# A decoder trunk's layer norms: last column block of the second rows in two banks, first scaling in halves, constant products taken out

## The chip, the cores and the metric

The kernel runs on one core of one Trainium2 chip. The metric is the device time of one execution in microseconds. An execution that the hardware profiler recorded gives the rows that are quoted below. Engines are called as the profile calls them: PE multiplies matrices, DVE and ACT work elementwise on 128 partitions, POOL does small things here, SP issues the transfers. PE writes into PSUM, which is used here as eight banks of 512 float32 columns.

## The reference

One sequence of 256 rows by 2048 columns goes through two layers. Each layer has a token mixer (forgetting attention in layer 0, sliding-window attention in layer 1) and a gated convolutional feed-forward part with 5632 inner columns. Around every one of these four parts stands the same frame:

```python
for i in range(DEPTH):                       # 2 layers
    mod = c_act @ ada_w[i] + ada_b[i]
    sh1, sc1, g1, sh2, sc2, g2 = jnp.split(mod[:, None, :], 6, axis=-1)
    h = x * (1.0 + sc1) + sh1
    y = fox_attention(h, ...) if i % 2 == 0 else swa_attention(h, ...)
    x = layer_norm(DEEPNORM_ALPHA * x + (1.0 + g1) * y, ln_mix_g[i], ln_mix_b[i])
    h = x * (1.0 + sc2) + sh2
    y = conv_ffn(h, ...)                     # h @ w_up, causal conv, silu(g) * val, @ w_down
    x = layer_norm(DEEPNORM_ALPHA * x + (1.0 + g2) * y, ln_ffn_g[i], ln_ffn_b[i])
```

The layer norm takes mean and variance over the 2048 columns of a row, so nothing of the next part can start before the last column of the last product of the part before it is known. The change concerns these four places.

## The kernel before

The 256 rows lie as two row tiles of 128 (t = 0 and 1; "the second rows" are t = 1) in a tile `x`. Weights come from memory in pieces of 256 rows by 512 columns, sixteen or more for one column block of a product. ACT casts each piece to a rounded part `wh` (L265), DVE forms the remainder `wl` (L276); `h` and `l` of a piece stand in one of four buffers. Every product is done three times, high by high, high by low and low by high, so the input of a product also comes as two tiles: `hH` (high, by ACT) and `hL` (low, by DVE; the profile names it `hH` as well).

There are two kinds of products. In `x_mm` the rows of the sequence are the stationary operand and 512 weight columns stream; its result is `xs`, one bank for each row tile. In `w_mm` the weights are stationary and 256 sequence rows stream; its result is `ws`. Input columns go by groups k of 128, sixteen in all; a weight piece covers two of them. The last column block of a part that ends in a layer norm uses `x_mm_end`: it finishes the products of the first rows and keeps those of the second rows back for the last two or four pieces, so that the evacuation of t = 0 runs beside the products of t = 1.

`residual` evacuates a column block: gate times product (L625), added to `x` (L627), and bn_stats (L632). After the last block follow bn_aggr (L635), the addition of epsilon (L637) and the power -1/2 on POOL (L638), which gives `rs`. A product of mean and `rs` for t = 0 (L631, on DVE) is the bias for ACT.

`between` stands at three of the four norms, here called seams: after the mixer of layer 0 (about 471 us), after its feed-forward part (about 1215 us) and after the mixer of layer 1 (about 1477 us). The fourth norm ends the kernel: there `residual` is followed by two operations with the norm's weights (L1173, L1174) and the output's transfers. A seam issues, in this order: a few products of constants whose result nobody reads (`spin(o, 3)`), the scaling of the first 512 columns, d = 0, of both rows (`normalise`: t = 0 on ACT, L648, t = 1 on DVE, L650), transposes of columns k = 0 to 3 (`mod_turn`, L489), `mod_pair` for them (high part straight from the bank on ACT, L499; the same affine on DVE, L500; the difference as low part, L501), and `spin(o, 2)`. The other columns come as `feeds`: after each weight piece one more pair of k goes through transposes and `mod_pair` (ACT L503, DVE L504, then the split into high and low at L84 and L85), and at k = 4, 8 and 12 the scaling of the next 512 columns goes ahead. In the forms of the first two feeds the word is `fast`.

Each engine works through its own queue in the order in which it was written by a scheduler. The scheduler may move an instruction ahead or behind others by its estimate of times, except where `pin` keeps it in the order of the program. So the text of the program doesn't tell the order of a queue; the rows of the queues do.

Of the kernel before, what the change touches and what calls it, by code (L numbers as in the profile page):

```python
# [41 lines left out]
def hybrid_trunk(ctx: ExitStack, tc: tile.TileContext, a: dict, out: bass.AP):  # L42
# [22 lines left out]
    def bank(name="sm"):  # L65
        return psp.tile([P, 512], F32, tag="ps", name=name)
# [1 line left out]
    def w_banks():  # L68
        return [bank("ws").rearrange("p (a s) -> p a s", a=2) for _ in range(2)]

    def x_banks():
        return [bank("xs") for _ in range(NT)]

    def mm(o, lhsT, rhs, start=False, stop=False, **kw):
        return nc.tensor.matmul(o, lhsT, rhs, start=start, stop=stop, **kw)  # L75

    def pin(ins, on=True):

        if on:
            tc.keep_in_program_order(ins)  # L80
# [214 lines left out]
    def x_mm_end(ps, stat, nk, n):  # L295

        kept = []

        def use(kc, h, l):
            end = kc >= nk - 2 * n  # L300
            x_mm(ps, kc, h, l, stat, nk - 1, ts=(0,) if end else range(NT))
            if end:
                kept.append((kc, h, l))
            if kc + 2 >= nk:
                for e in kept:
                    x_mm(ps, *e, stat, nk - 1, ts=(1,))

        return use

# [9 lines left out]

    def x_stationary(wsrc, col, k0, nk, stat, end=0):  # L320

        ps = x_banks()
# [148 lines left out]


    hpad = cst.tile([P, 2 * KC * S + 64], F32R, name="hH")
    hH = hL = None

    def place(o):
# [13 lines left out]
            os.append(o)  # L490
        return os

    def mod_pair(G, B, k, ps, fast=False, keep=False):
        tmp = ttile()
        if fast:
            for j in range(2):
                o = tmp[:, j * S:(j + 1) * S]
                g, b = G[:, k + j:k + j + 1], B[:, k + j:k + j + 1]
                pin(nc.scalar.activation(hH[:, k + j, :], ps[j], AF.Identity, bias=b, scale=g), keep)  # L499
                nc.vector.tensor_scalar(o, ps[j], g, b, op0=ALU.mult, op1=ALU.add)  # L500
                nc.vector.tensor_tensor(hL[:, k + j, :], o, f32(hH[:, k + j, :]), op=ALU.subtract)  # L501
            return
        pin(nc.scalar.activation(tmp[:, :S], ps[0], AF.Identity, bias=B[:, k:k + 1], scale=G[:, k:k + 1]), keep)  # L503
        nc.vector.tensor_scalar(tmp[:, S:], ps[1], G[:, k + 1:k + 2], B[:, k + 1:k + 2],  # L504
                                op0=ALU.mult, op1=ALU.add)
        split(hH[:, k:k + 2, :], hL[:, k:k + 2, :], tmp.rearrange("p (j s) -> p j s", j=2))
# [4 lines left out]
    def spin(o, n):  # L511

        for _ in range(n):
            pin(mm(o[:, :3 * P], ident, mask.rearrange("p a b -> p (a b)"), start=True, stop=True))

    def modulate(G, B, norm, o=None):

        def feed(k):
            if k % 4 == 0:
                norm(k // 4)  # L520
            mod_pair(G, B, k, mod_turn(k, 2), k < 4)

        feeds.extend([lambda k=k: feed(k) for k in range(0, KC, 2)])
        for _ in range(2):
            feeds.pop(0)()
        spin(o, 2)

    def opening(plan, proj, prep):

# [83 lines left out]
                prep()  # L613


    stats = cst.tile([P, NT, D // 512, nc.vector.BN_STATS_DIM], F32, name="stats")
    mhalf = cst.tile([P, 1], F32, name="mhalf")
    nc.gpsimd.memset(mhalf, -0.5)

# [2 lines left out]
    def residual(ps, d, gate, last):  # L622
        for t in range(NT):
            tmp = ttile()
            nc.vector.tensor_tensor(tmp, ps[t], gate[:, d * 512:(d + 1) * 512], op=ALU.mult)  # L625
            xs = x[:, t, d * 512:(d + 1) * 512]
            nc.vector.tensor_tensor(xs, xs, tmp, op=ALU.add)  # L627
            if last:
                if t == 1 and d == D // 512 - 1:
                    mu, rs, nm = moments[0]  # L630
                    pin(nc.vector.scalar_tensor_tensor(nm, mu, -1.0, rs, op0=ALU.mult, op1=ALU.mult))  # L631
                nc.vector.bn_stats(stats[:, t, d, :], xs)  # L632
                if d == D // 512 - 1:
                    mv = sp.tile([P, 2], F32, tag="mv", name="mv")
                    nc.vector.bn_aggr(mv, stats[:, t].rearrange("p a b -> p (a b)"))  # L635
                    rs = sp.tile([P, 2], F32, tag="rs", name="rs")
                    nc.vector.tensor_scalar_add(mv[:, 1:2], mv[:, 1:2], EPS)  # L637
                    nc.gpsimd.tensor_tensor(rs[:, 0:1], mv[:, 1:2], mhalf, op=ALU.pow)  # L638
                    moments[t] = (mv[:, 0:1], rs[:, 0:1], rs[:, 1:2])
            yield  # L640

    def normalise(d):

        for t in range(NT):
            mu, rs, nm = moments[t]
            xs = x[:, t, d * 512:(d + 1) * 512]
            if t == 0:
                nc.scalar.activation(xs, xs, AF.Identity, scale=rs, bias=nm)  # L648
            else:
                nc.vector.tensor_scalar(xs, xs, mu, rs, op0=ALU.subtract, op1=ALU.mult)  # L650

    def ln_rows(name, l):
        gb, bb = [], []
# [89 lines left out]
    def out_proj(oT, full, w_o, l):  # L743
        def stat(kc, t):
            while kc not in full:
                step()
            return oT[kc][0][:, t * P:(t + 1) * P], oT[kc][1][:, t * P:(t + 1) * P]

        ps = {d: x_banks() for d in range(2)}

        def part(d, ks):
            use = x_mm_end(ps[d], stat, KC, 2) if d == D // WB - 1 else                 lambda kc, h, l_: x_mm(ps[d], kc, h, l_, stat, KC - 1)
            stream(w_o, 0, d * WB, ks, use)

        for i, ks in enumerate((range(0, 8), range(8, 12))):
            then(lambda i=i: ada.update(rate=(1.3, 0.65)[l]))
            for d in range(2):
                part(d, list(ks))
        then(lambda: (ada_need(l, 2), ada.update(rate=(1.3, 0.75)[l])))
        for d in range(D // WB):  # L760
            if d < 2:
                part(d, list(range(12, KC)))
            else:
                ps[d] = x_banks()
# [437 lines left out]
```

## Time and profile before

| | us |
|---|---|
| runs | 2218.73 to 2219.84, median 2218.89 |
| the profiled execution | 2223.02 |
| its span | 2221.3 |
| PE busy | 2170.6 (98%) |
| DVE busy | 1784.0 (80%) |
| ACT busy | 1151.8 (52%) |
| POOL busy | 19.0 (1%) |

A row of the time line reads: start and duration in us, engine, line of the code, operation, output tile from input tiles, shapes, how many instructions were put together in the row, and in brackets the idle time of the engine ahead of it with the work that ended it. A row that puts together several reaches from the start of the first to the end of the last. The durations of neighbours overlap, since engines are pipelined. A row of stretches gives from:to, length, busy time (and instructions) of PE, weight loads, DVE, ACT and POOL, the clock granted to PE, and share and rate of the transfers.

### The profile page before, as it was taken

To read this page: it belongs to the slowest core of one execution; us is meant where nothing else is said; L and a number is where in the kernel's file an instruction comes from. 1 tells how busy PE (TensorE), PEld (TensorE's weight loads), DVE (VectorE), ACT (ScalarE), POOL (GpSimd) and SP (SyncE) were. 2 spreads that over 40 slices of the span, in tenths; PEclk is the share of its full clock that TensorE was granted. 3 is DMA by queue.
4 is the path that set the end of the run, shared out by engine and by line. 5 is a ranking of instruction groups with operands and counts; after the bars stand their busy time and mean duration, and the time that the engine had idled before them with its cause. 6 is when DMAs were issued, how large, how long until landed. Compare 5 with 4: busy or idle time off the path is not lost. (4 is left out here: it accounts for less than half of the span.)

```text
span 2221.3 us, 38316 instructions
## 1 busy us (share of the span) xinstructions
PE 2170.6 (98%) x14915; PEld 1976.7 (89%) x14915; DVE 1784.0 (80%) x2442; ACT 1151.8 (52%) x1825; POOL 19.0 (1%) x48
## 2 busy tenths in 40 slices
PE   6999999999999999999999999999999999999997
PEld 5999888889999988999987877789999888999986
DVE  6879999979979989798797798779888555666756
ACT  3435655555555543555644567555555533555532
POOL 0000000000000000000000000000000000000000
PEclk9999999999999999999999999999999999999999
DMA  9999999969979999799797676668888556666563
GB/s 332 368 340 373 350 357 324 330 225 329 345 250 313 320 318 379 257 318 320 247 355 248 211 255 208 209 220 295 279 267 270 183 193 193 196 192 197 190 195 109
DMA packets 274247, 602.98 MB, mean 271 GB/s; under 512 B 21063, under 2 KB 29961, under 8 KB 273553
## 3 DMA queue, kind: packets, MB, share of 16 engines
q1 hardware_dynamic: 273008, 595.85, 78.5%
q0 software_dynamic: 1056, 4.69, 0.6%
q8 instruction: 116, 1.90, 0.3%
q14 instruction: 67, 0.54, 0.1%
HBM read 598.37 MB, written 2.10 MB: 270 GB/s over the span
## 5 line engine op out<-in xcount | busy, mean ns | idle before, releaser
L265 ACT CAST wh<-w 128x1024 fp32r<-128x1024 f32 x728 | 765.4, 1053 | 798.4 <-PE ws L75 262.8
L75 PE MATMUL ws<-hH,wh 128*128 128x256 f32 x6656 | 1154.5, 278 | 4.6 <-ACT hH L84 2.1
L276 DVE TENSOR_TENSOR wl<-w,wh 128x1024 fp32r<-128x1024 f32 x728 | 887.4, 1221 | 336.7 <-ACT wh L265 323.4
L75 PEld LDWEIGHTS ws<-hH,wh 128*128 128x128 f32 x6656 | 1010.6, 189 | 12.1 <-issue 3.6
L75 PE MATMUL ws<-hH,wl 128*128 128x256 f32 x3328 | 917.7, 277 | 4.2 <-DVE wl L276 4.1
L75 PEld LDWEIGHTS ws<-hH,wl 128*128 128x128 f32 x3328 | 627.4, 189 | 5.7 <-DVE wl L276 5.6
L75 PE MATMUL xs<-wh,gT 128*128 128x512 f32 x1408 | 435.4, 390 | 0.0
L75 PEld LDWEIGHTS xs<-wh,gT 128*128 128x128 f32 x1408 | 264.3, 188 | 55.2 <-ACT gT L84 0.3
L75 PE MATMUL xs<-wl,gT 128*128 128x512 f32 x704 | 273.8, 389 | 0.0
L75 PE MATMUL xs<-wh,hH 128*128 128x512 f32 x704 | 238.1, 404 | 0.2 <-ACT wh L265 0.2
L394 DVE SCALAR_TENSOR_TENSOR acc<-wa,cact,acc 128x1024 f32<-128x1024 f32 x180 | 228.4, 1278 | 0.0
L394 DVE SCALAR_TENSOR_TENSOR acc<-wa,cactp,acc 128x1024 f32<-128x1024 f32 x128 | 162.2, 1277 | 0.0
L75 PEld LDWEIGHTS xs<-wh,hH 128*128 128x128 f32 x704 | 131.3, 188 | 30.4 <-issue 1.3
L75 PEld LDWEIGHTS xs<-wl,gT 128*128 128x128 f32 x704 | 132.2, 188 | 27.2
L75 PE MATMUL xs<-wl,hH 128*128 128x512 f32 x352 | 139.0, 396 | 2.5 <-DVE wl L276 2.5
L1086 ACT ACTIVATE u<-ws,ccol 128x256 f32<-128x256 f32 x176 | 96.8, 562 | 60.2 <-PE ws L75 45.3
L75 PE MATMUL xs<-wh,oT 128*128 128x512 f32 x384 | 125.7, 396 | 0.8 <-ACT oT L84 0.8
L1087 DVE SCALAR_TENSOR_TENSOR u<-ws,ccol,u 128x255 f32<-128x255 f32 x176 | 82.6, 477 | 15.9 <-ACT u L1086 15.6
L75 PEld LDWEIGHTS xs<-wh,oT 128*128 128x128 f32 x384 | 72.1, 188 | 16.7 <-ACT oT L84 1.2
L1089 DVE SCALAR_TENSOR_TENSOR u<-ws,ccol,u 128x254 f32<-128x254 f32 x176 | 83.0, 477 | 2.2
L75 PEld LDWEIGHTS xs<-wl,hH 128*128 128x128 f32 x352 | 66.4, 189 | 17.6 <-DVE wl L276 3.8
L569 DVE SCALAR_TENSOR_TENSOR oacc<-wo,cact,oacc 128x1024 f32<-128x1024 f32 (+1 forms) x68 | 73.3, 1079 | 8.7 <-DMA wo<-in_ada_w_dram 7.6
(215 smaller groups left out, 1269.0 us busy)
## 6 DMA issues: line engine op xcount, KB each, us to landing
w<-in_ffn_w_up_dram SPq DMA_DIRECT2D x352, 512.0 KB, 4.7
wa<-in_ada_w_dram SPq DMA_DIRECT2D x320, 512.0 KB, 5.6
w<-in_ffn_w_down_dram SPq DMA_DIRECT2D x176, 512.0 KB, 5.0
w<-in_fox_w_in_dram SPq DMA_DIRECT2D x96, 512.0 KB, 7.0
wo<-in_ada_w_dram SPq DMA_DIRECT2D x48, 512.0 KB, 9.5
w<-in_swa_w_in_dram SPq DMA_DIRECT2D x40, 512.0 KB, 4.5
w<-in_fox_w_o_dram SPq DMA_DIRECT2D x32, 512.0 KB, 6.3
w<-in_swa_w_o_dram SPq DMA_DIRECT2D x32, 512.0 KB, 5.0
```

What stands on the lines that cost most here:

```text
L75: return nc.tensor.matmul(o, lhsT, rhs, start=start, stop=stop, **kw)
L265: pin(nc.scalar.copy(h, w), False)
L276: pin(nc.vector.tensor_tensor(l, w, f32(h), op=ALU.subtract), behind[0] > 0)
L394: pin(nc.vector.scalar_tensor_tensor(ac, wo, (cactp if row else cact)[:, k:k + 1], ac, op0=ALU.mult, op1=ALU.add), True)
L569: nc.vector.scalar_tensor_tensor(acc, w[:, k], cact[:, kc:kc + 1], acc, op0=ALU.mult, op1=ALU.add)
L1086: nc.scalar.activation(u, pf, AF.Identity, bias=cw(CW, f), scale=cw(2, f))
L1087: nc.vector.scalar_tensor_tensor(u[:, 1:], pf[:, :S - 1], cw(1, f), u[:, 1:], op0=ALU.mult, op1=ALU.add)
L1089: nc.vector.scalar_tensor_tensor(u[:, 2:], pf[:, :S - 2], cw(0, f), u[:, 2:], op0=ALU.mult, op1=ALU.add)
```

## The change

In a part's last column block, when it is ended by `x_mm_end`, the second rows' product goes into two banks of 256 columns, named `xh`. `x_mm_end` issues for the second rows all kept products of the first half and then all of the second half. `residual` takes each half for itself (gate, addition, bn_stats); bn_aggr then reads five entries for t = 1. The constant product of mean and `rs` moves from DVE to POOL, right behind the power. `normalise` is pinned, and for t = 1 the first 512 columns are scaled as two halves. In the `mod_pair` of k = 0 to 3 the two DVE steps are pinned. `spin(o, 2)` goes, `spin(o, 3)` stays. A tile of 48 floats keeps the later tiles' addresses at a distance of 256 bytes from where they were.

```diff
-    def x_banks():
-        return [bank("xs") for _ in range(NT)]
+    def x_banks(halved=False):
+        return [bank("xs")] + [[bank("xh")[:, :WB // 2] for _ in range(2)] if halved else bank("xs")]
+
+    def pieces(o):
+        return [(p, slice(n * WB // 2, (n + 1) * WB // 2)) for n, p in enumerate(o)] if isinstance(o, list) \
+            else [(o, slice(0, WB))]
...
-    def x_mm(ps, kc, h, l, stat, last, first=0, ts=range(NT)):
+    def x_mm(ps, kc, h, l, stat, last, first=0, ts=range(NT), part=slice(0, 2)):
...
-                mm(ps[t], xh, h[:, i, :], start=kc + i == first)
-                mm(ps[t], xh, l[:, i, :])
-                mm(ps[t], xl, h[:, i, :], stop=kc + i == last)
+                for o, c in pieces(ps[t])[part]:
+                    mm(o, xh, h[:, i, c], start=kc + i == first)
+                    mm(o, xh, l[:, i, c])
+                    mm(o, xl, h[:, i, c], stop=kc + i == last)
...
-                for e in kept:
-                    x_mm(ps, *e, stat, nk - 1, ts=(1,))
+                for p in range(2):
+                    for e in kept:
+                        x_mm(ps, *e, stat, nk - 1, ts=(1,), part=slice(p, p + 1))
...
+    cst.tile([P, 48], F32, name="pad")
...
-                nc.vector.tensor_scalar(o, ps[j], g, b, op0=ALU.mult, op1=ALU.add)
-                nc.vector.tensor_tensor(hL[:, k + j, :], o, f32(hH[:, k + j, :]), op=ALU.subtract)
+                pin(nc.vector.tensor_scalar(o, ps[j], g, b, op0=ALU.mult, op1=ALU.add), fixed)
+                pin(nc.vector.tensor_tensor(hL[:, k + j, :], o, f32(hH[:, k + j, :]), op=ALU.subtract), fixed)
...
-            mod_pair(G, B, k, mod_turn(k, 2), k < 4)
+            mod_pair(G, B, k, mod_turn(k, 2), k < 4, False, k < 4)
...
-        spin(o, 2)
...
+            for n, (o, c) in enumerate(pieces(ps[t])):
+                cx = slice(d * 512 + c.start, d * 512 + c.stop)
+                xs = x[:, t, cx]
+                nc.vector.tensor_tensor(tmp[:, c], o, gate[:, cx], op=ALU.mult)
+                nc.vector.tensor_tensor(xs, xs, tmp[:, c], op=ALU.add)
+                if last:
+                    nc.vector.bn_stats(stats[:, t, d + n, :], xs)
...
+                if t == 0:
+                    nc.gpsimd.tensor_scalar(rs[:, 1:2], mv[:, 0:1], rs[:, 0:1], -1.0, op0=ALU.mult, op1=ALU.mult)
...
-                nc.scalar.activation(xs, xs, AF.Identity, scale=rs, bias=nm)
+                pin(nc.scalar.activation(xs, xs, AF.Identity, scale=rs, bias=nm))
             else:
-                nc.vector.tensor_scalar(xs, xs, mu, rs, op0=ALU.subtract, op1=ALU.mult)
+                for xp in ([xs[:, :S], xs[:, S:]] if d == 0 else [xs]):
+                    pin(nc.vector.tensor_scalar(xp, xp, mu, rs, op0=ALU.subtract, op1=ALU.mult))
```

What this does to the queues shows at the first seam. The line numbers of the changed kernel are higher: its L635, L636, L638, L641 and L643 are L625, L627, L632, L635 and L637 of the kernel before, L659 is L650, L507 and L508 are L500 and L501, L280 is L276, L511 is L504 and L89 is L85. DVE's queue from the first rows' evacuation to the second feed's low half, before:

```order
L625 TENSOR_TENSOR t<-xs,gate 128x512
L627 TENSOR_TENSOR x<-x,t 128x512
L631 SCALAR_TENSOR_TENSOR rs<-mv,rs 128x1
L632 BN_STATS stats<-x 128x6
L635 BN_AGGR mv<-stats 128x2
L637 TENSOR_SCALAR mv<-mv 128x1
L650 TENSOR_SCALAR x<-x,mv,rs 128x512 x4
L500 TENSOR_SCALAR t<-sm,G,B 128x256 x2
L501 TENSOR_TENSOR hH<-t,hH 128x256 x2
L500 TENSOR_SCALAR t<-sm,G,B 128x256 x2
L501 TENSOR_TENSOR hH<-t,hH 128x256 x2
L276 TENSOR_TENSOR wl<-w,wh 128x1024 x2
L504 TENSOR_SCALAR t<-sm,G,B 128x256
L276 TENSOR_TENSOR wl<-w,wh 128x1024
L85 TENSOR_TENSOR hH<-t,hH 128x512
```

(the first of these rows is that of the second rows), and now, from the first half scaling on:

```order
L659 TENSOR_SCALAR x<-x,mv,rs 128x256 x2
L507 TENSOR_SCALAR t<-sm,G,B 128x256
L508 TENSOR_TENSOR hH<-t,hH 128x256
L507 TENSOR_SCALAR t<-sm,G,B 128x256
L508 TENSOR_TENSOR hH<-t,hH 128x256
...
L280 TENSOR_TENSOR wl<-w,wh 128x1024 x2
L659 TENSOR_SCALAR x<-x,mv,rs 128x512
L280 TENSOR_TENSOR wl<-w,wh 128x1024
L511 TENSOR_SCALAR t<-sm,G,B 128x256 x2
L280 TENSOR_TENSOR wl<-w,wh 128x1024
L89 TENSOR_TENSOR hH<-t,hH 128x512 x2
```

The scalings of d = 1 to 3 have left the place ahead of the first low parts; affine step and low part alternate; and ahead of the second feed's low half now stand a scaling, two more steps and one remainder. The evacuation itself, now (two halves of `xh` and the first rows' moments between them):

```order
L635 TENSOR_TENSOR t<-xs,gate 128x512
L636 TENSOR_TENSOR x<-x,t 128x512
L635 TENSOR_TENSOR t<-xh,gate 128x256
L638 BN_STATS stats<-x 128x6
L636 TENSOR_TENSOR x<-x,t 128x256
L641 BN_AGGR mv<-stats 128x2
L638 BN_STATS stats<-x 128x6
L643 TENSOR_SCALAR mv<-mv 128x1
L635 TENSOR_TENSOR t<-xh,gate 128x256
L636 TENSOR_TENSOR x<-x,t 128x256
L638 BN_STATS stats<-x 128x6
L641 BN_AGGR mv<-stats 128x2
```

The first half is evacuated between the steps of the first rows. ACT's queue at the same seam, before:

```order
L648 ACTIVATE x<-x,rs 128x512 x3
L499 ACTIVATE hH<-sm,B,G 128x256 x4
L648 ACTIVATE x<-x,rs 128x512
L503 ACTIVATE t<-sm,B,G 128x256 x2
L265 CAST wh<-w 128x1024
L84 CAST hH<-t 128x512
```

and now (L656 is L648, L506 is L499, L510 is L503, L269 is L265, L88 is L84):

```order
L656 ACTIVATE x<-x,rs 128x512
L506 ACTIVATE hH<-sm,B,G 128x256 x4
L656 ACTIVATE x<-x,rs 128x512
L269 CAST wh<-w 128x1024
L656 ACTIVATE x<-x,rs 128x512
L510 ACTIVATE t<-sm,B,G 128x256
L269 CAST wh<-w 128x1024
L88 CAST hH<-t 128x512
```

The first rows' scalings of d = 1 and 2 now stand behind the first high parts, and a second cast of weights stands ahead of the second feed's high part. SP's queue is the same in both.

More of the change, by code (lines that the diff above doesn't have):

```diff
@@ L613, in opening @@
                 prep()
-    stats = cst.tile([P, NT, D // 512, nc.vector.BN_STATS_DIM], F32, name="stats")
+    stats = cst.tile([P, NT, D // 512 + 1, nc.vector.BN_STATS_DIM], F32, name="stats")
     mhalf = cst.tile([P, 1], F32, name="mhalf")
@@ L624, in residual @@
             tmp = ttile()
[L625 to L639, printed above, removed]
+            end = d == D // 512 - 1
+            for n, (o, c) in enumerate(pieces(ps[t])):
[5 more added lines that the diff above has]
+                    nc.vector.bn_stats(stats[:, t, d + n, :], xs)
+            if last and end:
+                mv = sp.tile([P, 2], F32, tag="mv", name="mv")
+                nc.vector.bn_aggr(mv, stats[:, t, :d + 1 + t].rearrange("p a b -> p (a b)"))
+                rs = sp.tile([P, 2], F32, tag="rs", name="rs")
+                nc.vector.tensor_scalar_add(mv[:, 1:2], mv[:, 1:2], EPS)
+                nc.gpsimd.tensor_tensor(rs[:, 0:1], mv[:, 1:2], mhalf, op=ALU.pow)
+                if t == 0:
+                    nc.gpsimd.tensor_scalar(rs[:, 1:2], mv[:, 0:1], rs[:, 0:1], -1.0, op0=ALU.mult, op1=ALU.mult)
+                moments[t] = (mv[:, 0:1], rs[:, 0:1], rs[:, 1:2])
             yield
```

6 lines of the change are left out of this document (3 added, 3 removed).

## The prediction

> **What bounds the kernel now.** I read the busy shares first, then the engines' time lines around the four layer norms, then the granted clock there.
>
> ```profile
> span 2221.3 us, 38316 instructions
> PE 2170.6 (98%) x14915; PEld 1976.7 (89%) x14915; DVE 1784.0 (80%) x2442; ACT 1151.8 (52%) x1825; POOL 19.0 (1%) x48
> 580.00:600.00 20.00, 20.00 (x179) 20.00 (x178) 19.96 (x28) 12.20 (x19) 0.00 (x0) 1.00 0.92 324
> 1120.00:1140.00 20.00, 20.00 (x89) 16.29 (x88) 20.00 (x24) 8.31 (x10) 0.00 (x0) 1.00 0.98 346
> ```
>
> PE is busy for 98% of the span: elsewhere it streams without a gap, 179 products of 256 columns in 20 us (112 ns each) or 89 of 512 (225 ns). So time can change only where PE waits: at the three seams (a layer norm followed by first transposes, near 471, 1215 and 1477 us) and in the last 15 us. The whole time of the profiled execution is 2223.02, 1.7 over its span and 4.1 above the median of the runs, 2218.89. The sum is made against 2223.02 and carried over to the median.
>
> The first seam on DVE, which turns the last product into moments, normalised rows and low halves (start, duration, line, tile):
>
> ```profile
> 469.28 0.69 DVE L625 TENSOR_TENSOR t<-xs,gate 128x512 f32<-128x512 f32 x1 [3.21 <-PE xs L75]
> 470.01 0.69 DVE L627 TENSOR_TENSOR x<-x,t 128x512 f32<-128x512 f32 x1
> ...
> 472.08 0.69 DVE L625 TENSOR_TENSOR t<-xs,gate 128x512 f32<-128x512 f32 x1 [0.17 <-PE xs L75]
> 472.81 0.69 DVE L627 TENSOR_TENSOR x<-x,t 128x512 f32<-128x512 f32 x1
> 473.42 0.15 DVE L631 SCALAR_TENSOR_TENSOR rs<-mv,rs 128x1 f32<-128x1 f32 x1
> 473.53 0.69 DVE L632 BATCH_NORM_STATS2 stats<-x 128x6 f32<-128x512 f32 x1
> 474.26 0.26 DVE L635 BATCH_NORM_AGGREGATE mv<-stats 128x2 f32<-128x24 f32 x1
> 474.56 0.15 DVE L637 TENSOR_SCALAR mv<-mv 128x1 f32<-128x1 f32 x1
> 475.38 1.92 DVE L650 TENSOR_SCALAR x<-x,mv,rs 128x512 f32<-128x512 f32 x4 [0.67 <-POOL rs L638]
> 477.22 0.99 DVE L500 TENSOR_SCALAR t<-sm,G,B 128x256 f32<-128x256 f32 x2
> 478.12 0.75 DVE L501 TENSOR_TENSOR hH<-t,hH 128x256 fp32r<-128x256 f32 x2
> 478.79 1.00 DVE L500 TENSOR_SCALAR t<-sm,G,B 128x256 f32<-128x256 f32 x2
> ...
> 480.36 2.36 DVE L276 TENSOR_TENSOR wl<-w,wh 128x1024 fp32r<-128x1024 f32 x2
> 482.63 0.54 DVE L504 TENSOR_SCALAR t<-sm,G,B 128x256 f32<-128x256 f32 x1
> 483.09 1.22 DVE L276 TENSOR_TENSOR wl<-w,wh 128x1024 fp32r<-128x1024 f32 x1
> 484.22 0.69 DVE L85 TENSOR_TENSOR hH<-t,hH 128x512 fp32r<-128x512 f32 x1
> 474.80 0.55 POOL L638 TENSOR_TENSOR rs<-mv,mhalf 128x1 f32<-128x1 f32 x1 [2.23 <-DVE mv L637]
> ```
>
> From 475.38 to 484.91 DVE has no gap: its one wait is that for POOL's power. PE beside it:
>
> ```profile
> 471.65 0.39 PE L75 MATMUL xs<-wh,hH 128*128 128x512 f32 x1
> 471.88 2.10 PE L75 MATMUL spin<-mask,ident 128*128 128x384 f32 x6
> ...
> 475.99 0.66 PE L489 MATMUL sm<-ident,x 128*128 128x128 f32 x4 [0.85 <-DVE x L650]
> 476.48 1.46 PE L75 MATMUL spin<-mask,ident 128*128 128x384 f32 x4
> ...
> 478.01 0.82 PE L489 MATMUL sm<-ident,x 128*128 128x128 f32 x6
> 478.60 0.38 PE L75 MATMUL ws<-hH,wh 128*128 128x256 f32 x1
> ...
> 484.96 0.39 PE L75 MATMUL ws<-hH,wh 128*128 128x256 f32 x1
> ```
>
> The product at 478.60 is the first that needs a low half (the first L501 ends .06 earlier: the two stand .33 apart, 478.12 to 478.79, so one takes .75 - .33 = .42). At 484.96 PE waits a second time, for the low halves of k 4 and 5 (L85, ended 484.91). So two things on DVE set a seam: when its chain starts, and how much stands ahead of the L85 of the second feed.
>
> **The change part by part.** *Products in halves.* 432 products of 256 columns replace 216 of 512: 432 x .1117 - 216 x .2247 = -0.3 by the windows above. I take 0; if the second weight load showed it would be more, but the 256-wide window has 178 loads in 20 us without a gap.
>
> *Evacuation in halves.* A dependent step on DVE costs its duration plus .03 (469.28 to 470.01); an independent one about .61 (472.81 to 473.42). A step of 256 columns takes .42 and stands .33 from the next, by L501. The moments of t0 now share the queue with the first half of t1: gate t0 469.28, x 470.01, gate h1 470.69, stats t0 471.02, x h1 471.63, aggregate 471.96, stats h1 472.14, mv t0 472.49; then gate h2 472.60, x 473.06, stats 473.51, aggregate 473.98, mv ends 474.43. Before, it ended at 474.71: the halves win 0.3, not the half of an evacuation, because the queue is full. A half's stats appear in no row; I take .43, between .30 (half of .61) and .61, which moves the end by -.1 to +.2.
>
> *The constant product to POOL.* It frees .11 of DVE; t0's second POOL operation I take at .28 by
>
> ```profile
> 4.08 0.28 POOL L127 TENSOR_SCALAR cactp<-cact 128x16 f32<-128x16 f32 x1
> 476.35 1.93 ACT L499 ACTIVATE hH<-sm,B,G 128x256 fp32r<-128x256 f32 x4 [0.52 <-PE sm L489]
> ```
>
> (bound .55, the power's row). ACT's scaling of t0 hangs on it, but its transposes come before those of t1, for which PE idles .85 (475.99). Cost 0.
>
> *First scaling in halves.* Power 474.51 to 475.07, first half 475.10 to 475.51, so t1's transposes start at 475.57 against 475.99: -0.4 (a half's scaling .41, between .27 and .57).
>
> *Scalings of d 1 to 3 later, first low halves in a fixed order.* ACT's hH of k 0 starts .36 after the first transpose (475.99 to 476.35) and takes .56 (1.93 for four that stand .457 apart, as scalings on DVE do: 1.92 for four): 476.50. L507 now reads the same bank behind it: 476.54. Its low half runs 477.11 to 477.53, and PE's first waiting product starts at 477.59 instead of 478.60: -1.0. The six transposes at 478.01 (.65 by their starts), which lay in that wait, now come behind it: net -0.35.
>
> From there DVE is gapless. Each t and its low half now depend on one another: .54 + .03 + .33 = .90, four times 3.62, where t, t, low, low took (480.36 - 477.22)/4 = .785 each, 3.14. Then: 480.16; two weight residuals (1.135 each, 480.36 to 482.63) 482.43; the scaling of d 1 (.457, a fourth of the x4 row's start to 477.22) 482.89; a residual 484.02; two L511 (.46 each, 482.63 to 483.09) 484.93; a residual 486.07; L89 to 486.76. Before, one L504 and one residual stood between the pair of residuals and L85; now a scaling, two residuals and two L511 do. The product of k 4 starts at 486.81 against 484.96: **+1.85**. PE covers nothing of it, since before it already stood waiting there; the high halves of k 4 come late as well, as ACT's second cast (L269) is now ahead of L88. At k 8 a further scaling (.457) stands ahead of L89, on ACT another ahead of L88: +0.5. So a seam into a 256-column product costs **+2.4**. Bounds: -0.35, if PE found cover in its products; +2.9, if the scalings of k 12 (.457) showed too.
>
> *The other seams.* The third has the same kind of product behind it and the same second wait:
>
> ```profile
> 1488.59 0.68 DVE L85 TENSOR_TENSOR hH<-t,hH 128x512 fp32r<-128x512 f32 x1
> 1489.33 0.38 PE L75 MATMUL ws<-hH,wh 128*128 128x256 f32 x1
> 1222.64 0.68 DVE L85 TENSOR_TENSOR hH<-t,hH 128x512 fp32r<-128x512 f32 x1
> 1223.10 0.80 PE L75 MATMUL xs<-wh,hH 128*128 128x512 f32 x1
> ```
>
> +2.4 there too. The second seam feeds 512-column products, whose order (high, residual, low) asks for the low half of k 4 later: PE begins k 4 at 1223.10 without waiting on L85. What decides there is the high half from ACT, which I work out at 1224.4: +1.3, less .4 of a drain that no longer stands next to it: **+0.9** (bounds 0 and 2.4).
>
> *The tail.* There is no transpose behind the last norm, and DVE is gapless:
>
> ```profile
> 2202.01 0.69 DVE L625 TENSOR_TENSOR t<-xs,gate 128x512 f32<-128x512 f32 x1 [3.13 <-PE xs L75]
> ...
> 2216.05 1.41 DVE L1174 SCALAR_TENSOR_TENSOR x<-x,rs,ln 128x512 f32<-128x512 f32 x2
> ```
>
> Each step that is cut in two adds a start (.06 net, three steps), and the first L1183 may wait for POOL's power: **+0.2** (0 to +0.4).
>
> *Constant products out.* The four records at 476.48 filled PE's wait; they end before 478.60, so nothing is won. Without them PE streams less there:
>
> ```profile
> 77.64:81.05 3.41, 3.41 (x33) 3.41 (x32) 0.61 (x1) 2.80 (x3) 0.00 (x0) 1.00 1.05 386
> 81.05:87.88 6.83, 6.83 (x33) 6.83 (x33) 3.89 (x6) 0.65 (x2) 0.00 (x0) 0.50 0.97 330
> 473.59:477.00 3.41, 2.06 (x12) 1.30 (x11) 2.67 (x7) 2.88 (x5) 0.55 (x1) 1.00 0.00 0
> ```
>
> (The column after POOL's is the granted clock; clock changes lie on a grid of 3.41 us.) At 77.64 PE was counted busy throughout, but from 78.92 on with products of one column; the next 6.83 us ran at half clock. In 473.59:477.00 it streamed 8 transposes and two constant products, .47 of the stretch at .109 and .32 each, and the clock stayed. Without them the worst stretch holds 8 transposes and two products: 8 x .109 + 2 x .113 = 1.10 us, .32. That lies under the share that lost the clock (1.28 of 3.41, .38), for about three phases of the grid in ten at the first and third seams.
>
> The page "TensorE: Matmul & The Clock Gate" of the Trainium skill, in Part 1, says that half rate comes after an idle window of about 3.4 us, free-running. By it alone no clock would be lost here, since PE never idles that long at a seam, and the sum would stand; the trace differs, as the stretch at 77.64 lost the clock while PE was counted busy.
>
> **Sum.** 2.4 + 0.9 + 2.4 + 0.2 = +5.9: the profiled time goes from 2223.02 to 2228.9, the median from 2218.89 to **2224.8** (+0.27%).
>
> **Rivals.** *A clock drop.* One at the first or third seam runs up to 6.83 us of products at half rate; the waits for DVE absorb most, as PE waits about 2 us of it and DVE sets the pace: +0.95 each (0 to 1.7). 2225.7 for one, 2226.7 for both. For it: the streamed share. Against it: the phase must fit.
>
> *Not slower.* The second wait at k 4 decides. If PE reaches k 4 as late as DVE does (that is, if its products and transposes run 1.85 longer up to there), the gain of the start remains: from that point on a seam is worth -0.35 to -1.0, and three with the tail give 2216 to 2218. Against it: PE stood still at 484.96 already.
>
> *A smaller loss.* If the scheduler's rows run as listed but ACT and DVE overlap better (the t and low half pairs at .785 as before: -.5 a seam; no k 8 wait: -.5), each ws seam costs +1.4, and the sum is +3.2: 2222. That the change doesn't bring the moments forward by what halves promise is already in the sum (0.3).
>
> **Numbers.** Within 0.2% (4.4 us: 2214.5 to 2223.3) a measurement of this kernel can hardly tell a change from none. Forecast without a drop .47; a drop .27; the smaller loss .14; not slower .12. The range 2221.0 to 2227.2 leaves out most of "not slower" and the ends of the others, 2 in 10. Faster by over 0.2% .04, the far end of "not slower"; within 0.2% .22 (the rest of it, the smaller loss); slower .74.
>
> **What would show it.** At the first seam in the changed profile: first half scaling near 475.1, first product with a low half near 477.6, DVE without a gap until 486.8, and PE idle ahead of k 4 until then. Wrong if PE is not idle there, if L89 of k 4 ends before 485.5, or if the granted clock falls below 1 at a seam (then the rival).

## The result

The changed kernel takes 2228.18 us (median of 5 runs, 2226.83 to 2232.78); the kernel before took 2219.49 beside it (5 runs, 2218.73 to 2223.27). The ratio is 1.0043, with a 95% interval of 1.0032 to 1.0053: slower, by more than the forecast 2224.8 and just outside its range. The profiled execution took 2230.66 with a span of 2228.9, so the spans differ by 7.6.

The whole time of either kernel varies by some 5 us from run to run, and the traces show where: in the first 165 us some stretches run at half clock, most of them while PE waits for the first inputs, and how many and how long differs from execution to execution. Behind them the traces are steady to a few hundredths. So the whole times say that the kernel is slower, and the place of the loss is read from stages. A stage's length is the distance between two of ACT's 728 casts of weights, which all kernels here issue in the same order. The first seam, for instance, is taken from the 113th to the 166th cast; these rows of the time line, of before, are its ends:

```profile
415.92 1.05 ACT L265 CAST wh<-w 128x1024 fp32r<-128x1024 f32 x1
...
575.12 1.06 ACT L265 CAST wh<-w 128x1024 fp32r<-128x1024 f32 x1 [1.66 <-PE ws L75]
```

and of after:

```profile
412.86 1.05 ACT L269 CAST wh<-w 128x1024 fp32r<-128x1024 f32 x1
...
576.12 1.06 ACT L269 CAST wh<-w 128x1024 fp32r<-128x1024 f32 x1 [1.66 <-PE ws L79]
```

163.26 against 159.20: +4.06. The changed kernel came to this stage 3.05 earlier, by the luck of the opening, which is why its span shows only 7.6. (Of all traces here the one of before has the slowest opening.) All stages in the same way, in us over the kernel before (113, 166, 385, 411, 456, 491 and 716 are the bounding casts; the tail goes to the end of the span):

| stage | forecast | after |
|---|---|---|
| opening, to cast 113 | 0 | -3.05 |
| first seam, 113 to 166 | +2.4 | +4.05 |
| 166 to 385 | 0 | -0.04 |
| second seam, 385 to 456 | +0.9 | +1.76 |
| third seam, 456 to 491 | +2.4 | +4.09 |
| 491 to 716 | 0 | 0.00 |
| tail, from 716 | +0.2 | +0.82 |
| sum without the opening | +5.9 | +10.7 |

The loss lies at the four places that were forecast and nowhere else, and at each of them it is larger. DVE at the first seam of the changed kernel:

```profile
466.80 0.69 DVE L635 TENSOR_TENSOR t<-xs,gate 128x512 f32<-128x512 f32 x1 [3.30 <-PE xs L79]
467.52 0.69 DVE L636 TENSOR_TENSOR x<-x,t 128x512 f32<-128x512 f32 x1
468.23 0.43 DVE L635 TENSOR_TENSOR t<-xh,gate 128x256 f32<-128x256 f32 x1
468.57 0.68 DVE L638 BATCH_NORM_STATS2 stats<-x 128x6 f32<-128x512 f32 x1
...
470.92 0.43 DVE L638 BATCH_NORM_STATS2 stats<-x 128x6 f32<-128x256 f32 x1
471.38 0.29 DVE L641 BATCH_NORM_AGGREGATE mv<-stats 128x2 f32<-128x30 f32 x1
471.71 0.15 DVE L643 TENSOR_SCALAR mv<-mv 128x1 f32<-128x1 f32 x1
472.53 0.74 DVE L659 TENSOR_SCALAR x<-x,mv,rs 128x256 f32<-128x256 f32 x2 [0.67 <-POOL rs L644]
473.97 0.54 DVE L507 TENSOR_SCALAR t<-sm,G,B 128x256 f32<-128x256 f32 x1 [0.70 <-ACT hH L506]
474.55 0.42 DVE L508 TENSOR_TENSOR hH<-t,hH 128x256 fp32r<-128x256 f32 x1
474.89 0.54 DVE L507 TENSOR_SCALAR t<-sm,G,B 128x256 f32<-128x256 f32 x1
...
482.16 0.55 DVE L511 TENSOR_SCALAR t<-sm,G,B 128x256 f32<-128x256 f32 x1 [0.58 <-PE sm L496]
483.09 0.54 DVE L511 TENSOR_SCALAR t<-sm,G,B 128x256 f32<-128x256 f32 x1 [0.38 <-PE sm L496]
483.55 1.22 DVE L280 TENSOR_TENSOR wl<-w,wh 128x1024 fp32r<-128x1024 f32 x1
484.69 1.52 DVE L89 TENSOR_TENSOR hH<-t,hH 128x512 fp32r<-128x512 f32 x2
```

From the end of x (L636, 468.21) the rows are within about .1 of the forecast ladder: half stats .43 as taken, t and low half .92 apart (forecast .90), the first half scaling .82 behind the start of the moments' last step (L643), as before. The wait of .70 for the first high part lies in the ladder too (first scaling done, 476.54 for L507). What is not in it are the waits of .58 and .38 for transposes of k 4. PE beside it:

```profile
469.80 1.77 PE L79 MATMUL spin<-mask,ident 128*128 128x384 f32 x5
472.02 0.66 PE L496 MATMUL sm<-ident,x 128*128 128x128 f32 x4 [0.44 <-ACT x L656]
473.00 0.76 PE L496 MATMUL sm<-ident,x 128*128 128x128 f32 x4 [0.33 <-DVE x L659]
473.99 0.50 PE L79 MATMUL ws<-hH,wh 128*128 128x256 f32 x2 [0.23 <-ACT hH L506]
475.03 0.58 PE L79 MATMUL ws<-hH,wh 128*128 128x256 f32 x1 [0.54 <-DVE hH L508]
475.41 0.42 PE L79 MATMUL ws<-hH,wl 128*128 128x256 f32 x1
475.62 0.63 PE L79 MATMUL ws<-hH,wh 128*128 128x256 f32 x2
...
484.42 0.50 PE L79 MATMUL ws<-hH,wh 128*128 128x256 f32 x2 [0.93 <-ACT hH L88]
485.43 0.39 PE L79 MATMUL ws<-hH,wh 128*128 128x256 f32 x1 [0.50 <-DVE hH L89]
```

Two things in it were not in the sum. From 475.03 on products stand .21 apart instead of .113 (475.41 to 475.62), which is half clock; the transposes of k 4 (481.74, 482.67) come behind these products without a gap on PE, more than 1 us after the scaling that they read (L659 at 479.90, .54 long). So it is the slowed PE that DVE waits for there, and not the late scaling; where the clock stays (constant products back, below), DVE does not wait there. And further up the block of half products is longer than the block of whole ones was; that shows below.

PE waits twice for k 4 here, .93 and .50. The kernel before did not wait there, though the prediction reads its row at 484.96 so:

```profile
484.47 0.71 PE L489 MATMUL sm<-ident,x 128*128 128x128 f32 x5
484.96 0.39 PE L75 MATMUL ws<-hH,wh 128*128 128x256 f32 x1
```

The five transposes ran up to the product, the last from 484.91 on, when L85 ended. PE and DVE arrived together, by chance, so every delay of DVE from there on still shows in full.

### The profile page after: what moved, and what is told of

It is laid out like the page before. It is cut to its first block, busy times and chain, and to the rows that moved or that the text cites. A ratio compares the mean times of both kernels' runs of the same rounds, so it can differ in the third digit from the quotient of the medians.

```text
span 2228.9 us, 38746 instructions
## 1 busy us (share of the span) xinstructions
PE 2174.3 (98%) x15119; PEld 1986.1 (89%) x15119; DVE 1786.5 (80%) x2453; ACT 1151.6 (52%) x1825; POOL 21.0 (1%) x52
## 4 chain that ended last, share of the span: by engine, by line
PE 77%; DVE 11%; issue 5%; DMA 3%; ACT 3%; POOL 0%; SPq 0%; DVEq 0%; ACTq 0%; POOLq 0%
PE ws L79 44%; PE xs L79 28%; DVE wl L280 3%; DVE acc L400 3%; PE xh L79 2%; DMA wo<-in_ada_w_dram 1%; ACT wh L269 1%; PE sm L79 1%; DMA wa<-in_ada_w_dram 1%; PE sm L438 0%; DMA w<-in_fox_w_in_dram 0%; PE cps L79 0%; PE S L79 0%; DVE oacc L575 0%; DVE pr L707 0%
## 5 line engine op out<-in xcount | busy, mean ns | idle before, releaser
L269 ACT CAST wh<-w 128x1024 fp32r<-128x1024 f32 x728 | 764.9, 1052 | 809.7 <-PE ws L79 291.1
L280 DVE TENSOR_TENSOR wl<-w,wh 128x1024 fp32r<-128x1024 f32 x728 | 887.5, 1222 | 339.0 <-ACT wh L269 319.6
L79 PE MATMUL xs<-wh,gT 128*128 128x512 f32 x1328 | 413.2, 390 | 0.0
L79 PEld LDWEIGHTS xs<-wh,gT 128*128 128x128 f32 x1328 | 249.4, 188 | 51.7 <-ACT gT L88 0.3
L79 PE MATMUL xs<-wl,gT 128*128 128x512 f32 x664 | 258.4, 389 | 0.0
L79 PE MATMUL xs<-wh,hH 128*128 128x512 f32 x688 | 233.4, 404 | 1.4 <-ACT hH L88 1.2
L79 PEld LDWEIGHTS xs<-wl,gT 128*128 128x128 f32 x664 | 124.7, 188 | 25.0
L79 PE MATMUL xs<-wh,oT 128*128 128x512 f32 x336 | 112.2, 397 | 0.8 <-ACT oT L88 0.8
L79 PEld LDWEIGHTS xs<-wh,oT 128*128 128x128 f32 x336 | 63.2, 188 | 14.5 <-ACT oT L88 1.3
```

The source lines that it names most:

```text
L269: pin(nc.scalar.copy(h, w), False)
L280: pin(nc.vector.tensor_tensor(l, w, f32(h), op=ALU.subtract), behind[0] > 0)
```

## Undoing one part at a time

Stage sums leave out the opening, as above. All kernels compute what the reference does.

**The half products back to whole ones** (evacuation whole too):

```diff
-        ps = x_banks(end > 0)
+        ps = x_banks()
...
-                ps[d] = x_banks(d == D // WB - 1)
+                ps[d] = x_banks()
```

> The changed kernel with the last block's second rows in one bank of 512 columns again, so with 512-column products and whole evacuation; all else as changed. The changed kernel's trace has the half products 120 ns apart, not the 113 I took: theory P (products) says 432 x .120 - 216 x .2267 = 2.9 us come back, less up to .3 a seam for the later moments, so about 2 us under the changed kernel's 2228.2: 2226. The recorded prediction's theory (halves are free and win .3 a seam) says about 1 us over it: 2229.

Ratio to before 1.0037 [1.0024, 1.0050]. Stages: first seam +3.50, second +1.19, third +3.89, tail -0.08, sum 8.5: 2.2 less than the changed kernel, as theory P says. The whole times (2229.77) can't tell 2 us with five runs. Half products cost, and in this pair they cost most in the tail (.9). The part of each stage that lies ahead of the first rows' gate product (L635, the first step of the evacuation) shows it without anything else in it: in the changed kernel it is .57, .80, .48 and .60 longer than in the kernel before at the four norms, 2.45 in all, and with whole products it is as long as before within .01.

**The constant products back:**

```diff
         for _ in range(2):
             feeds.pop(0)()
+        spin(o, 2)
```

> The changed kernel with the constant products behind the first transposes put back. Theory C (clock) says that the two stretches of half clock at the first and third seams go, since PE then streams about .7 of the stretch, and with them .5 to 1 us each: 2226.5 to 2227.5, and granted clock 1.00 throughout 470 to 490 and 1475 to 1495. The rival, that PE's pace there is hidden behind DVE, says 2228.2 although the clock stays.

Ratio 1.0030 [1.0018, 1.0042]. First seam +2.94, third +2.91, second +1.95: 1.1 and 1.2 less where the changed kernel had lost the clock, .2 more where it had not: 2.1 in all. The stretches around the two losses, of the changed kernel:

```profile
471.44:474.85 3.41, 2.05 (x11) 1.11 (x10) 1.97 (x6) 2.00 (x5) 0.55 (x1) 1.00 0.02 5
474.85:478.26 3.41, 3.23 (x15) 3.23 (x16) 3.31 (x8) 1.16 (x2) 0.00 (x0) 0.50 0.00 0
478.26:481.67 3.41, 3.41 (x31) 3.41 (x31) 3.32 (x4) 1.77 (x2) 0.00 (x0) 1.00 0.46 168
1481.78:1485.20 3.42, 2.02 (x11) 1.22 (x11) 2.02 (x6) 2.08 (x5) 0.55 (x1) 1.00 0.00 0
1485.20:1488.61 3.41, 3.41 (x16) 3.41 (x17) 3.31 (x7) 0.87 (x2) 0.00 (x0) 0.50 0.00 0
```

and with the constant products back:

```profile
474.23:477.64 3.41, 3.41 (x25) 2.89 (x24) 3.27 (x8) 2.04 (x4) 0.00 (x0) 1.00 0.02 5
```

So the rival of the clock drop is real: 15 and 16 products in a stretch where the next has 31. This run also shows what the ladder of the prediction is worth where the clock stays (its L636, L511 and L89 are L635, L511 and L89 of the changed kernel):

```profile
467.06 0.69 DVE L636 TENSOR_TENSOR t<-xs,gate 128x512 f32<-128x512 f32 x1 [3.30 <-PE xs L79]
481.76 1.06 DVE L511 TENSOR_SCALAR t<-sm,G,B 128x256 f32<-128x256 f32 x2
483.87 1.51 DVE L89 TENSOR_TENSOR hH<-t,hH 128x512 fp32r<-128x512 f32 x2
```

DVE has no gap from the first low part to here. The first of the two L89 ends 17.49 behind the first gate product; the ladder has 17.48 (486.76 against 469.28), the kernel before 15.63, the changed kernel 18.57.

**The scalings not pinned:**

```diff
-                pin(nc.scalar.activation(xs, xs, AF.Identity, scale=rs, bias=nm))
+                nc.scalar.activation(xs, xs, AF.Identity, scale=rs, bias=nm)
...
-                    pin(nc.vector.tensor_scalar(xp, xp, mu, rs, op0=ALU.subtract, op1=ALU.mult))
+                    nc.vector.tensor_scalar(xp, xp, mu, rs, op0=ALU.subtract, op1=ALU.mult)
```

> The changed kernel with the layer norm's scalings not pinned: the scheduler puts those of d 1 to 3 ahead of the first low parts again. Theory Q (queue: what stands ahead of the second feed's low half on DVE costs) says the 1.85 at k 4 and the .5 at k 8 go at the first and third seams and .9 at the second, so 4 to 5.5 us less than changed: 2223 to 2224, the first low part 1.4 us later than in the changed kernel, and the wait at k 4 about as before the change. The rival (products and clock hold the loss) says 2227 or more.

2219.86 against 2220.84, ratio 0.9997 [0.9989, 1.0006]. First seam -0.46, second +0.18, third +0.23, tail +0.82: the loss is gone but for the tail. The undoing gives back 9.9, where theory Q had 4 to 5.5. The clock stayed, which is 2.1 of it, and the scalings alone cost 5.4 (below); the other 2.4 belong to no single part. The half products and the earlier start still stand in the seams; why they cancel here and not in the changed kernel was not taken apart. DVE's only wait in 468 to 485 is again the one for the power:

```profile
DVE x L659 <- POOL rs L644: 0.7, 1, 0.7
```

**The pairs not fixed:**

```diff
-            mod_pair(G, B, k, mod_turn(k, 2), k < 4, False, k < 4)
+            mod_pair(G, B, k, mod_turn(k, 2), k < 4, False, False)
```

> The changed kernel with affine step and low part of the first four k not pinned: their order is again two affine steps, two low parts. Theory Q says .12 less for each of four on a gapless DVE, .5 a seam, so 2226.7; if a wait for transposes stands behind them on DVE instead (the changed kernel's trace shows DVE waiting for PE's transposes of k 4), it is hidden and 2228.2 stays.

Ratio 1.0035 [1.0023, 1.0047]. Stages -.4, -.2 and -.2 against the changed kernel, .8 in all where theory Q had 1.5. At the first seam DVE waits .3 for a high part of the second feeds (L89 for L88), where the changed kernel had no such wait; that part of the saving is lost.

## One part alone, in the kernel before

**The scalings pinned, nothing else:**

```diff
-                nc.scalar.activation(xs, xs, AF.Identity, scale=rs, bias=nm)
+                pin(nc.scalar.activation(xs, xs, AF.Identity, scale=rs, bias=nm))
...
-                nc.vector.tensor_scalar(xs, xs, mu, rs, op0=ALU.subtract, op1=ALU.mult)
+                pin(nc.vector.tensor_scalar(xs, xs, mu, rs, op0=ALU.subtract, op1=ALU.mult))
```

> The kernel before with the layer norms' scalings pinned alone, so that those of d 1 to 3 go behind weight work. Theory Q (DVE's queue): about +2 to +2.5 us at the first and third seam and +.9 at the second, 5 to 6 us slower than before, tail unchanged; the clock stays at 1.00, since the constant products are there. The rival, that pinning alone is harmless without the fixed pairs and halves: within 1 us.

Ratio 1.0027 [1.0018, 1.0037]. First seam +2.30, second +0.81, third +2.33, tail 0.01, and no half clock: the sizes forecast for the whole change at the seams (2.4, 0.9, 2.4), from this part alone. DVE's waits in 469.5 to 486, where the kernel before had only the third:

```profile
DVE t L500 <- ACT hH L499: 1.0, 1, 1.0
DVE t L504 <- PE sm L489: 0.9, 1, 0.9
DVE x L650 <- POOL rs L638: 0.7, 1, 0.7
DVE wl L276 <- ACT wh L265: 0.2, 1, 0.2
```

The new waits add up to 2.1, about the 2.3 that are lost; over 26 us behind the moments DVE waits 4.0 us here and 1.7 in the kernel before, 2.3 more. DVE does the same work in either kernel; the early scalings had filled its time while it waited for the first high part.

**The halves alone:** products, evacuation and bn_stats in halves, nothing pinned.

```diff
-        ps = x_banks()
+        ps = x_banks(end > 0)
...
-                ps[d] = x_banks()
+                ps[d] = x_banks(d == D // WB - 1)
...
+            for n, (o, c) in enumerate(pieces(ps[t])):
```

> The kernel before with the halves alone (products, evacuation and bn_stats of the last block's second rows); nothing pinned, constant products and order as before. Theory P (a half product costs 120 ns where half of a whole one costs 113): +.65 in each block of 96 products and +.8 in each of 120, 2.9 in all, less about .3 at each of three seams for the earlier moments: 2 us slower than before, .9 of it in the tail. The recorded theory (halves free): .9 us faster at the seams, the tail the same within .2.

Ratio 1.0005 [0.9997, 1.0014]. First seam +0.20, second +0.85, third +0.72, tail +0.89: 2.6 in all. Theory P had 2; the earlier moments win even less than the .3 a seam.

**The stationary operand shared by both halves:** in the changed kernel, the two halves' products with one operand follow each other.

```diff
-                for o, c in pieces(ps[t])[part]:
-                    mm(o, xh, h[:, i, c], start=kc + i == first)
-                    mm(o, xh, l[:, i, c])
-                    mm(o, xl, h[:, i, c], stop=kc + i == last)
+                for w_, v_, f_ in ((xh, h, 0), (xh, l, 1), (xl, h, 2)):
+                    for o, c in pieces(ps[t])[part]:
+                        mm(o, w_, v_[:, i, c], start=f_ == 0 and kc + i == first, stop=f_ == 2 and kc + i == last)
```

> The changed kernel with the products of the two halves issued next to one another for each stationary operand, where both halves are issued together. If the 120 ns come from loading a stationary operand for half the columns, two products that share it should come down to 113 ns; if they come from the moving operand or the bank, 120 stays.

120 ns stay (median between starts), and the stages are those of the changed kernel within .06. So it isn't the change of operand from one product to the next. The loads themselves are not ruled out: each product still has a load of its own, 15119 loads beside 15119 products in both traces.

**Half products into one bank,** with nothing else changed:

```diff
+                for n in range(2):
+                    c = slice(n * WB // 2, (n + 1) * WB // 2)
+                    mm(ps[t][:, c], xh, h[:, i, c], start=kc + i == first and n == 0, skip_group_check=True)
+                    mm(ps[t][:, c], xh, l[:, i, c], skip_group_check=True)
+                    mm(ps[t][:, c], xl, h[:, i, c], stop=kc + i == last, skip_group_check=True)
```

> The kernel before with nothing changed but that the last block's products of the second rows are issued as halves of 256 columns into the two halves of their one bank; evacuation whole, order as before. If it is the narrow product itself that costs, the halves stand 120 ns apart here too and the block is .7 to .9 us longer at each of the four norms, about 3 us in all, the tail included; if it is the second bank, they come at 113 ns and nothing changes.

First seam +0.56, second +0.95, third +0.67, tail +0.79: 3.0 for the products alone. The narrow product is what costs, not the second bank. In the last block before the tail they run like this (first rows and last of a row of 36 products):

```profile
2202.02 0.40 PE L75 MATMUL xs<-wh,gT 128*128 128x256 f32 x2
2202.26 0.28 PE L75 MATMUL xs<-wl,gT 128*128 128x256 f32 x1
2202.38 0.40 PE L75 MATMUL xs<-wh,gT 128*128 128x256 f32 x2
...
2206.22 0.28 PE L75 MATMUL xs<-wl,gT 128*128 128x256 f32 x1
```

Three in .36. Whole ones stood 226.7 apart in the kernel before, so each half costs 6 to 7 ns more than half, .6 and .75 in blocks of 96 and 120; the rest is that the first rows' whole products between them stand 226 to 236 apart, 231 in the mean, instead of 227. Beside that, `ws` products of the same width run 113 ns apart (the row 580:600 of the prediction). Why the two kinds differ stays open.

**The constant products out alone:**

```diff
         for _ in range(2):
             feeds.pop(0)()
-        spin(o, 2)
```

> The kernel before with the constant products behind the first transposes taken out alone. Theory C (a stretch of 3.41 us in which PE streams under about .38 loses the clock): without the four records the worst stretch at the first and third seam has .2 to .3 for most phases, so half clock there and +.5 to +1.1 each. If it is the pinned scalings that bring the drop, no drop and 0.

Against the expectation: no half clock at the first and third seam, and .26 and .21 won there; but half clock at the second, +0.95:

```profile
1208.20:1211.66 3.46, 1.78 (x11) 1.18 (x11) 2.73 (x8) 2.94 (x6) 0.55 (x1) 1.00 0.00 0
1211.66:1215.07 3.41, 3.41 (x13) 2.93 (x12) 3.41 (x9) 2.76 (x6) 0.00 (x0) 0.50 0.00 0
470.96:474.37 3.41, 2.22 (x15) 1.41 (x13) 2.82 (x7) 2.89 (x7) 0.55 (x1) 1.00 0.00 0
```

Counted in streamed columns (113 ns for 256, 227 for 512, 109 for a transpose, 322 for a constant product), the stretch ahead of 1211.66 has .33 of its length, the one ahead of 474.37 .43. Over all traces here, every stretch at a seam with .35 or less was followed by half clock (eight of them) and every one with .41 or more was not; of three with .39, two were. Whether a stretch falls so depends on where the grid lies against the seam. In the changed kernel the first transposes of the first and third seam are 1010.1 us apart, close to 296 periods of 3.413 (1010.3), so the two seams meet the grid alike: both lost the clock there and in three of its variants (whole products, pairs not fixed, operand shared). In the kernel before they are 1004.3 apart, 294.2 periods.

## Tries at a faster version

**d 1 scaled early, d 2 and 3 behind the low halves** (whole products, constant products in, pairs free, the scalings pinned in this new order):

```diff
-            if k % 4 == 0:
-                norm(k // 4)
-            mod_pair(G, B, k, mod_turn(k, 2), k < 4, False, k < 4)
+            if k == 0:
+                norm(0)
+                norm(1)
+            mod_pair(G, B, k, mod_turn(k, 2), k < 4)
+            if k in (4, 8):
+                norm(k // 4 + 1)
```

> A version drawn from these results: whole products and evacuation, first scaling in halves, constant products kept, pairs not fixed; of the scalings d 1 stands right behind d 0, where DVE waits for ACT's first high part, and d 2 and d 3 come behind the low halves of k 4 and k 8. Theory Q: the second wait shrinks by the two scalings taken out of it (.9) and the start keeps its .4: 1 to 1.5 us less than before at the first and third seam, 0 to .5 at the second, tail as before: 2 to 3 us faster than before, which is less than 0.2%. If only the total of DVE's work mattered and not its order: no change.

Missed: +0.19, +0.09, +0.19, tail -0.05, ratio 1.0000 [0.9991, 1.0008]. The low half of k 4 does come .4 earlier after the seam's first gate product, but the scalings put behind it delay the next ones by as much. Theory Q in the form that only the queue ahead of k 4 counts falls. DVE is behind for longer than that: in the kernel before its next wait for transposes comes at 490.88, 16 us behind the moments, and up to there the total of its work and waits counts.

**Scalings of the second rows' d 2 and 3 on ACT** (and the product of mean and power of both rows on POOL):

```diff
-            if t == 0:
+            if t == 0 or d >= 2:
                 nc.scalar.activation(xs, xs, AF.Identity, scale=rs, bias=nm)
```

> The kernel before with the second rows' scalings of d 2 and 3 on ACT instead of DVE, and the products of mean and power for both rows on POOL. Theory W (a seam is as long as DVE's work in it plus DVE's idle time; in the earlier version with d 1 early the order alone won nothing): DVE loses .91 + .15 of work in each seam, so about 1 us less at the first and third seam and up to .5 at the second, 2 to 2.5 us faster in all, tail as before. The rival, that PE's second wait hangs on ACT's high parts, says 0 or slower, since ACT has more to do.

Missed as well: +0.26, +0.20, +0.81, ratio 1.0008 [0.9999, 1.0017]. DVE has 1 us less to do in a seam and waits more, since ACT's scalings now stand ahead of its first high part: over 26 us behind the moments 2.8, 4.1 and 3.4 at the three seams, where the kernel before has 1.7, 3.1 and 1.7. At the first seam:

```profile
DVE t L504 <- PE sm L489: 1.2, 2, 0.9
DVE t L500 <- ACT hH L499: 0.9, 1, 0.9
DVE x L648 <- POOL rs L635: 0.7, 1, 0.7
```

**d 1 on ACT too, first scaling in halves:**

```diff
-            if t == 0:
+            if t == 0 or d >= 1:
                 nc.scalar.activation(xs, xs, AF.Identity, scale=rs, bias=nm)
...
+                for xp in (xs[:, :S], xs[:, S:]):
+                    nc.vector.tensor_scalar(xp, xp, mu, rs, op0=ALU.subtract, op1=ALU.mult)
```

> The same with the scalings of d 1 on ACT as well and the first one in halves. Theory W: another .46 of DVE's work less and the start .4 earlier, less about .2 for the wait on ACT's first high part and the extra start of a half: 1.5 us less than before at the first and third seam, .5 to 1 at the second, 3 to 4 us faster in all. The rival: ACT becomes the bound, little or nothing beyond the version with d 2 and 3 alone.

+0.09, +0.67, +0.74, ratio 1.0010 [1.0001, 1.0019]. Same reason: the wait for the first high part, 1.2, 1.8 and 1.8 at the three seams, takes back what DVE is spared.

**The changed kernel with whole products and free scalings:**

> The changed kernel with whole products and evacuation and scalings not pinned (constant products out, first scaling in halves, pairs fixed). Adding up the stages of the two single undoings: first seam -.5 - .5, second -.1 - .6 + .3, third +.2 - .2, tail .8 - .9: 1.5 us faster than before and no stretch of half clock, since with the scalings unpinned no phase of the grid had less than .43 streamed.

+0.85, +0.24, +0.55, tail -0.07, ratio 1.0006 [0.9997, 1.0015]; against the expectation half clock at the first seam, behind a stretch with .39. The stages of single undoings don't add up. No version beat the kernel before by what can be measured.

## Why the prediction was wrong

The stages split at the first rows' gate product tell the forecast's terms apart. Ahead of it only the products differ; behind it lies all that the ladder and the tail's term describe. In us over the kernel before:

| | forecast | constant products back, behind it | changed, behind it | changed, ahead of it |
|---|---|---|---|---|
| first seam | +2.4 | +2.37 | +3.49 | +.57 |
| second seam | +.9 | +1.16 | +.96 | +.80 |
| third seam | +2.4 | +2.42 | +3.60 | +.48 |
| tail | +.2 | +.23 | +.22 | +.60 |
| sum | +5.9 | +6.2 | +8.3 | +2.45 |

- **Products in halves: the step that failed.** "432 x .1117 - 216 x .2247 = -0.3 ... I take 0" took the spacing of 256-column `ws` products for `xs` products. They stand 120 ns apart instead of 113, and whole products between them came slower too. That is the last column, 2.45, where the forecast had 0; alone in the kernel before, half products cost 3.0.
- **The clock: a rival that happened.** It had .27 and 3 phases in 10, and no place in the sum. In the changed kernel it fell at both seams; leaving the constant products out cost 1.1 and 1.2 there against a price of .95, 2.1 in all with what the second seam gives back. The price was near by luck, as it was taken from up to 6.83 us of half clock and 3.41 came. That .38 loses the clock held, as stretches of .39 lost it in two of three cases; the number of phases was too low. In all four traces with the scalings pinned and the constant products out it fell at both seams, and the two seams share one phase. The rule of the page "TensorE: Matmul & The Clock Gate" of the Trainium skill, Part 1 (half rate after an idle window), would have given no drop; the trace has one after stretches in which PE was busy for 2.05 of 3.41 us, so what counts is less than full idleness.
- **The deferred scalings: right, in mechanism and size.** Where the clock stayed, the second column, the first and third seam came out within .03 of the forecast and k 4 within .01 of the ladder. (That run has the constant products in, which the forecast took as free; out alone they won .26 and .21 where the clock stayed, so the seams may be some .2 smaller without them.) One row was misread on the way: PE did not stand waiting at 484.96. It arrived there together with the low half, so that it could cover nothing, as the forecast had it; that was luck. It was no luck that PE then stood idle ahead of k 4, .93 and .50, against the rival "not slower". Pinning the scalings alone gave +2.30, +0.81 and +2.33; that this is near the forecast too is partly chance, since the forecast has the fixed pairs and the earlier start in it.
- **Earlier moments and first scaling: right and small.** From the first gate product to the end of the moments it took 5.06, forecast 5.15, before 5.43. The tail from its first gate product to DVE's end took 15.61 against 15.45.
- **The sum.** 5.9 as forecast, 2.45 for half products ahead of the evacuation and 2.1 for the clock make 10.5, of 10.7 measured. The sign held; of the two terms that were missing, either alone would have left the stages at 8.4 or 8.0 and both together took them to 10.7. The medians show 8.7, as the opening differs. This account holds for the changed kernel; that undoing the scalings gives back 9.9 shows that its parts lean on one another.

## What to carry to other kernels

A ladder of steps laid out from rows of the same kinds came out within some .2 us at two seams; the term that failed was taken from rows of another kind. Where one engine is short of time behind a barrier, look at its waits beside its queue: work that seems to stand in the way may be what fills a wait, and moving it away opens the wait without making the work less. A product cut in two isn't two half products: take its price from products of the same kind. Filler work on PE can be worth a microsecond even where it wins nothing by itself, if without it PE streams too little in a stretch of the clock's grid.

## What the runs showed of the hardware

- Products of 256 columns stood 120 ns apart with sequence rows stationary, in one bank or two, and 113 with weights stationary. Whole products between such halves came at 226 to 236 ns (mean 231) instead of 227. What makes the difference stays open.
- Half clock followed all eight stretches of 3.41 us at a seam with .35 or less streamed, though PE counted as busy for 60% of those in the changed kernel. It lasted 3.41 us; keeping PE streaming there saved 1.1 and 1.2.
- The share of half clock changes between executions of one kernel: of 29 runs of the kernel before, the fastest (2216.47) has a mean granted clock of .995 and the slowest (2223.95) .992. In all traces but for single stretches at the seams the half clock lies in the opening and behind the last products. An effect of 2 us is hard to see in whole times of such a kernel with 5 to 12 runs; the stages show it.
